# The SSD's y products of two pairs of heads run back to back, and the buffers around them change

## The chip, the cores and the metric

The kernel runs on one core of a Trainium2 chip. The metric is the device time of one execution in microseconds (us). A core has TensorE for matrix products (PE in the profile, PEld its loads of weights), VectorE (DVE), ScalarE (ACT), GpSimd (POOL), SyncE (SP), and DMA queues. Each engine works through its own instructions in the order in which the program has them; semaphores make one engine wait for another.

## The reference

One layer, float32, 272 tokens (16 meta tokens and 256 frames) of width 2048. What matters here is the SSD mixer in it: 64 heads of 64 channels in 8 groups, a state of 128.

```python
proj = xn @ w_in
sc_b, sc_c, sc_h, z, xbc, dt_raw, gate_raw = split_cols(proj, IN_SIZES)
xbc = jax.nn.silu(causal_dwconv(xbc, mb_conv_w, mb_conv_b))
xs, Bm, Cm = jnp.split(xbc, [D_INNER, D_INNER + D_BC], axis=-1)
...
decay = jnp.exp(jnp.where(causal, seg, -jnp.inf))
cb = jnp.einsum('bclgn,bcsgn->bcgls', Cc, Bc)
y_diag = jnp.einsum('bcgrls,bcsgrp->bclgrp', decay * cb[:, :, :, None], xdt)
...
y_m = (y_ssd + xs * d_skip[:, None].astype(xs.dtype)).reshape(bsz, L, D_INNER)
y_m = y_m * jax.nn.silu(z)
y_m = rmsnorm(y_m.reshape(bsz, L, MB_GROUPS, D_INNER // MB_GROUPS),
              mb_norm_g.reshape(MB_GROUPS, D_INNER // MB_GROUPS)).reshape(bsz, L, D_INNER)
```

After it come the two output projections, the gates, w_o, and an MLP of width 5504 with a convolution, all of which the change leaves alone. The kernel does the scan without chunks, as a masked product over all tokens: y = (decay * (C B)) x dt.

## The kernel before

Channels lie on the 128 partitions, tokens along the free dimension. A weight tile is 128 x 128; all products of the layer are one long list of jobs, and a job of the input projection is 16 such tiles, in two pieces of 8. A piece comes by DMA as float32 (raw), ScalarE rounds it to whi (line 115), VectorE computes the rest, wlo = raw - whi (line 116); PE then runs 16 matmuls with whi and 8 with wlo (lines 276 to 279). Four pairs of whi and wlo and five raw buffers run in a ring, so a cast for a piece waits until PE has finished the piece four before it.

The order on PE and on SP is the order in which the program is written. On the other engines a scheduler decides it when the program is built, and it is fixed then. What a job's result sets off later is put into a table by job number: after(delay, fn) runs fn when delay more jobs have been put on PE, ahead of that job's evacuation.

A group of eight heads (ssd_group, g = 0 to 7) has ten jobs: B, C, and four each of xs and z, alternating (in group 0 the z come earlier). A pair of heads fills 128 partitions, so a group has four pairs, i = 0 to 3. For pair i, after xs job: three jobs later xs_tr transposes xs on PE (L451, L452) into xd; one later decay(i) computes on GpSimd eight instructions (line 473) into the buffer m, from the rows qb that load_q brings; one later decay_exp(i) takes the exponential on ScalarE (L479) and multiplies by the masked C B, cbm, on VectorE (L480). Seven jobs after the xs job y_out(i) runs the y product on PE: for each of three blocks of tokens one matmul per head (L495), of 64 columns of weights each, into the two halves of one PSUM bank. The trace has two records for each of these float32 matmuls, so 12 for a pair. Then VectorE adds the skip (L497), GpSimd multiplies by silu(z) (L499), ScalarE squares, GpSimd adds the squares up in ss (L506). Two jobs after the last pair, y_norm sums ss over the partitions by a matmul on PE (ny, L512); VectorE and ScalarE make the reciprocal root of it, and GpSimd multiplies the group's four yf by it (L517). These steps of a group fall among the jobs of the next group. In the last group the delays are shorter.

The buffers: m has two, shared by all pairs; a decay can write one only after the y product that read it. qb has two, one per group. sqy, the square, has one.

Of the kernel before, what the change touches and what calls it, by code (L numbers as in the profile page):

```python
# [8 lines left out]
F32 = mybir.dt.float32  # L9
# [6 lines left out]
P = 128  # L16
# [3 lines left out]
T = SEQ + META  # L20
KD = D // P
HEADS = 64
GROUPS = 8
# [10 lines left out]
TR_DELAY, Y_DELAY = 3, 7  # L34
# [4 lines left out]
T_Y = 14  # L39
# [18 lines left out]
N0, N1, N2 = NY, T - 128, T - 256  # L58
NM = N0 + N1 + N2
L1 = 128 - T_Y  # L60
# [60 lines left out]
def block_kernel(ctx: ExitStack, tc: tile.TileContext, xT: bass.AP, par: bass.AP, w_in: bass.AP, w_a: bass.AP,  # L121
                 w_m: bass.AP, w_o: bass.AP, w_up: bass.AP, w_down: bass.AP, out: bass.AP):
    nc = tc.nc
# [39 lines left out]
    paux = ctx.enter_context(tc.tile_pool(name="paux", bufs=1, space=PSUM))  # L163
# [95 lines left out]
    def after(delay, fn):  # L259
        later.setdefault(state["job"] + delay, []).append(fn)  # L260
# [65 lines left out]
    sd = None  # L326
# [68 lines left out]
        after(5, transposes)  # L395

    def load_q(g):
        qb = sd.tile([P, 8, T], F32, tag="qb", name="qb", bufs=2)
        nc.gpsimd.dma_start(out=qb, in_=qd[8 * g:8 * g + 8, :].rearrange("h t -> (h t)").partition_broadcast(P)
                            .rearrange("p (h t) -> p h t", h=8))  # L400
        return qb

    def conv_silu(ps, j, c0, n, dst):

        e = sd.tile([P, T], F32, tag="e", name="e", bufs=2)
        nc.vector.tensor_tensor(out=e[:, c0:], in0=ps, in1=rstd[:, c0:], op=ALU.mult)
        a = 0 if c0 == 0 else T_Y
        u = sd.tile([P, T], F32, tag="u", name="u", bufs=2)
        nc.scalar.activation(out=u[:, a:], in_=e[:, a:], func=AF.Identity, scale=hc("mbw3", j), bias=hc("mbb", j))
        for s, w in ((1, "mbw2"), (2, "mbw1"), (3, "mbw0")):  # L410
            b = max(a, c0 + s)
            nc.vector.scalar_tensor_tensor(out=u[:, b:], in0=e[:, b - s:T - s], scalar=hc(w, j), in1=u[:, b:],
                                           op0=ALU.mult, op1=ALU.add)
        th = sd.tile([P, T], F32, tag="th", name="th", bufs=2)
        silu_of_half(dst[:, a:], u[:, a:], th[:, a:])

    def ssd_group(g):
        G = {}

        def b_evac(ps):  # L420
            G["B"] = Z["B"][g % 2]
            conv_silu(ps, 32 + g, 0, T, G["B"][:, :T])

        def c_evac(ps):
            G["C"] = sd.tile([P, T], F32, tag="C", name="C", bufs=2)
            conv_silu(ps, 40 + g, T_C, T - T_C, G["C"])
            after(2, cb)

        def cb():
            B, C = G["B"], G["C"]  # L430
            ps = paux.tile([P, 512], F32, tag="cb", name="cb")
            nc.tensor.matmul(ps[:, 0:N0], B[:, 0:128], C[:, T_Y:], start=True, stop=True)  # L432
            nc.tensor.matmul(ps[:, N0:N0 + N1], B[:, 128:256], C[:, 128:], start=True, stop=True)  # L433
            nc.tensor.matmul(ps[:, N0 + N1:NM], B[:, 256:], C[:, 256:], start=True, stop=True)  # L434
            m = G["cb"] = sd.tile([P, NM], F32, tag="cbm", name="cbm", bufs=2)
            nc.vector.tensor_tensor(out=m, in0=ps[:, :NM], in1=mask, op=ALU.mult)
            G["qb"] = load_q(g)

        def xs_evac(ps, i):
            j = 4 * g + i  # L440
            G["xs", i] = sd.tile([P, T], F32, tag=f"xs{i}", name="xs", bufs=2)
            conv_silu(ps, j, 0, T, G["xs", i])
            after(TR_DELAY if g < GROUPS - 1 else 2, lambda: xs_tr(i))
            after(Y_DELAY if g < GROUPS - 1 else 5, lambda: y_out(i))

        def xs_tr(i):
            j = 4 * g + i
            x = G["xs", i]
            ps = paux.tile([P, 512], F32, tag="tr", name="tr")
            for b in range(2):  # L450
                nc.tensor.transpose(ps[:, b * P:(b + 1) * P], x[:, b * P:(b + 1) * P], ident)  # L451
            nc.tensor.transpose(ps[:N2, 2 * P:3 * P], x[:, 256:], ident)  # L452
            xd = G["xd", i] = Z["xd"][i]
            tok = S["tok"]
            h = 2 * j
            nc.vector.tensor_tensor(
                out=xd[:, 0:2], in0=ps[:, :2 * P].rearrange("p (b h c) -> p b h c", b=2, h=2),
                in1=tok[:, :2 * HEADS].rearrange("p (b h) -> p b h", b=2)[:, :, h:h + 2].unsqueeze(3)
                .broadcast_to([P, 2, 2, 64]), op=ALU.mult)
            nc.vector.tensor_tensor(  # L460
                out=xd[:N2, 2], in0=ps[:N2, 2 * P:3 * P].rearrange("p (h c) -> p h c", h=2),
                in1=tok[:N2, 2 * HEADS + h:2 * HEADS + h + 2].unsqueeze(2).broadcast_to([N2, 2, 64]), op=ALU.mult)
            after(1, lambda: decay(i))

        def decay(i):
            tok, qb = S["tok"], G["qb"]
            m = G["m", i] = sd.tile([P, 2, NM], F32, tag="m", name="m", bufs=2)
            for a in range(2):
                hl = 2 * i + a
                h = 8 * g + hl  # L470
                q0, q1, q2, q0m = (tok[:, o * HEADS + h:o * HEADS + h + 1] for o in (3, 4, 5, 6))
                for c0, n, t0, q in ((0, L1, T_Y, q0), (L1, N1, 128, q0m), (N0, N1, 128, q1), (N0 + N1, N2, 256, q2)):
                    nc.gpsimd.tensor_scalar(out=m[:, a, c0:c0 + n], in0=qb[:, hl, t0:t0 + n], scalar1=q,  # L473
                                            scalar2=0.0, op0=ALU.subtract, op1=ALU.max)
            after(1, lambda: decay_exp(i))

        def decay_exp(i):
            m, cbm = G["m", i], G["cb"]
            nc.scalar.activation(out=m, in_=m, func=AF.Exp, scale=-1.0)  # L479
            nc.vector.tensor_tensor(out=m, in0=m, in1=cbm.unsqueeze(1).broadcast_to([P, 2, NM]), op=ALU.mult)  # L480

        def z_evac(ps, i):
            u = sd.tile([P, T], F32, tag="u", name="uz", bufs=2)[:, :NY]
            th = sd.tile([P, T], F32, tag="th", name="thz", bufs=2)[:, :NY]
            nc.vector.tensor_tensor(out=u, in0=ps, in1=rstdh[:, T_Y:], op=ALU.mult)
            G["sz", i] = sd.tile([P, NY], F32, tag=f"sz{i}", name="sz", bufs=1)
            silu_of_half(G["sz", i], u, th)

        def y_out(i):
            j = 4 * g + i  # L490
            xd, m = G["xd", i], G["m", i]
            y = paux.tile([P, 512], F32, tag="y", name="y", bufs=2)
            for b, c0, n, t0 in ((0, 0, N0, 0), (1, N0, N1, L1), (2, N0 + N1, N2, 256 - T_Y)):
                for a in range(2):
                    nc.tensor.matmul(y[64 * a:64 * a + 64, t0:t0 + n], xd[:, b, a, :], m[:, a, c0:c0 + n],  # L495
                                     start=b == 0, stop=b == 2)
            nc.vector.scalar_tensor_tensor(out=yf[j], in0=G["xs", i][:, T_Y:], scalar=pc("dskip", j), in1=y[:, :NY],  # L497
                                           op0=ALU.mult, op1=ALU.add)
            nc.gpsimd.tensor_tensor(out=yf[j], in0=yf[j], in1=G["sz", i], op=ALU.mult)  # L499
            if i == 0:  # L500
                G["ss"] = sd.tile([P, NY], F32, tag="ss", name="ss", bufs=1)
                nc.scalar.activation(out=G["ss"], in_=yf[j], func=AF.Square)
            else:
                sq = sd.tile([P, NY], F32, tag="sqy", name="sqy", bufs=1)
                nc.scalar.activation(out=sq, in_=yf[j], func=AF.Square)
                nc.gpsimd.tensor_tensor(out=G["ss"], in0=G["ss"], in1=sq, op=ALU.add)  # L506
            if i == 3:
                after(2 if g < GROUPS - 1 else 1, y_norm)

        def y_norm():  # L510
            ps = paux.tile([P, 512], F32, tag="misc", name="ny")[:, :NY]
            nc.tensor.matmul(ps, ones, G["ss"], start=True, stop=True)  # L512
            rs = sd.tile([P, NY], F32, tag="rs", name="rs", bufs=1)
            rsqrt_mean(rs, ps, 512, sd, "sqy")
            for i in range(4):
                j = 4 * g + i
                nc.gpsimd.tensor_tensor(out=yf[j], in0=yf[j], in1=rs, op=ALU.mult)  # L517

        in_product(J_B + g, 0, T, b_evac)
        in_product(J_C + g, T_C, T - T_C, c_evac)  # L520
        for b, i in group_order(g):
            if b == J_XS:
                in_product(b + 4 * g + i, 0, T, lambda ps, i=i: xs_evac(ps, i))
            else:
                in_product(b + 4 * g + i, T_Y, NY, lambda ps, i=i: z_evac(ps, i))
# [273 lines left out]
```

## Time and profile before

| | |
|---|---|
| median of 3 runs | 2131.57 us (2131.17 to 2131.7) |
| profiled execution | 2131.41 us |
| span of its instructions | 2129.7 us |
| PE busy | 2108.8 us, 99% of the span |
| PEld, DVE, ACT, POOL busy | 96%, 63%, 48%, 21% |
| mean granted TensorE clock | 0.997 of full speed |
| bytes read from HBM | 384.77 MB, 182 GB/s over the span |

The span runs from the first to the last instruction; the time of an execution has another 1.7 us around it. Busy shares are averages over the whole kernel. The SSD's groups run in the first 610 us of it; there POOL is busy for 314 us of the 540 between 60 and 600. Matmuls follow each other in a pipeline, so a record's duration is longer than the step to the next one; costs on PE are therefore read from starts. "L276 ... x8" in a timeline is eight records of that line in a row, merged, with the first one's start.

### The profile page before, as it was taken

How to read it: one execution, taken by the hardware profiler on the slowest of the kernel's cores; microseconds unless marked ns; L12 is line 12 of the kernel's file. 1: busy time of each engine (PE TensorE's matmuls, PEld its weight loads, DVE VectorE, ACT ScalarE, POOL GpSimd, SP SyncE). 2: the span in 40 equal slices, each digit the busy share in tenths (PEclk: the TensorE clock that was granted, in tenths of full speed). 3: DMA queues.
4: the chain of work that ended last, by engine and by line, in shares of the span. 5: the costliest groups of instructions: out<-in, count | busy, mean ns of one | idle time of the engine just before them, and what ended most of it. 6: DMA issues, size and time to landing. Idle time of an engine off the chain costs nothing.

```text
span 2129.7 us, 39486 instructions
## 1 busy us (share of the span) xinstructions
PE 2108.8 (99%) x16254; PEld 2035.5 (96%) x16254; DVE 1347.9 (63%) x1829; ACT 1015.6 (48%) x1317; POOL 449.8 (21%) x483
## 2 busy tenths in 40 slices
PE   8999999999999999999999999999999999999997
PEld 7999999999999999999999999999999999988887
DVE  8788888788774444555555555666666666655454
ACT  5455555555573333444444444555454454444442
POOL 4247555755710000000000002101111111100010
PEclk9999999999999999999999999999999999999999
DMA  7565555554446555555555556555555555556663
GB/s 235 199 196 178 164 184 180 180 180 159 158 159 202 185 182 185 182 186 180 187 180 186 180 184 222 182 184 184 183 188 182 185 185 182 188 180 184 192 188 118
DMA packets 108548, 389.50 MB, mean 183 GB/s; under 512 B 12352, under 2 KB 14656, under 8 KB 107344
## 3 DMA queue, kind: packets, MB, share of 16 engines
q1 hardware_dynamic: 105696, 374.96, 54.9%
q0 software_dynamic: 1952, 11.10, 1.5%
q8 instruction: 127, 2.08, 0.4%
q10 hardware_dynamic: 720, 0.93, 0.1%
q14 instruction: 53, 0.43, 0.1%
HBM read 384.77 MB, written 2.17 MB: 182 GB/s over the span
## 4 chain that ended last, share of the span: by engine, by line
PE 97%; DVE 1%; POOL 1%; issue 0%; ACT 0%; DVEq 0%; ACTq 0%; POOLq 0%
PE acc L279 32%; PE acc L277 24%; PE acc L276 24%; PE acc L274 15%; PE y L495 1%; DVE wlo L116 1%; PE tr L451 0%; POOL m L473 0%; DVE o L740 0%; PE cb L432 0%; PE ny L512 0%; PE tr L452 0%; POOL ss L506 0%; PE cb L433 0%; PE cb L434 0%
## 5 line engine op out<-in xcount | busy, mean ns | idle before, releaser
L115 ACT CAST whi<-raw 128x1024 fp32r<-128x1024 f32 (+1 forms) x724 | 744.5, 1030 | 971.9 <-PE acc L277 567.6
L116 DVE TENSOR_TENSOR wlo<-raw,whi 128x1024 fp32r<-128x1024 f32 (+1 forms) x724 | 883.1, 1221 | 453.3 <-ACT whi L115 426.9
L276 PE MATMUL acc<-xg,whi 128*128 128x258 f32 (+3 forms) x2576 | 646.2, 287 | 1.8 <-ACT whi L115 1.3
L277 PE MATMUL acc<-xg,whi 128*128 128x258 f32 (+3 forms) x2576 | 641.0, 284 | 3.6 <-DVE xg L205 3.6
L277 PEld LDWEIGHTS acc<-xg,whi 128*128 128x128 f32 x2576 | 485.1, 188 | 4.6 <-DVE xg L205 4.0
L276 PEld LDWEIGHTS acc<-xg,whi 128*128 128x128 f32 x2576 | 484.9, 188 | 3.4 <-ACT whi L115 2.4
L279 PE MATMUL acc<-xg,wlo 128*128 128x258 f32 (+3 forms) x2576 | 366.8, 284 | 3.1 <-DVE wlo L116 3.0
L279 PEld LDWEIGHTS acc<-xg,wlo 128*128 128x128 f32 x2576 | 335.6, 189 | 4.1 <-DVE wlo L116 4.1
L473 POOL TENSOR_SCALAR m<-qb,tok 128x144 f32<-128x144 f32 (+2 forms) x256 | 228.3, 909 | 108.1 <-PE y L495 100.3
L279 PE MATMUL acc<-hg,wlo 128*128 128x256 f32 (+1 forms) x1376 | 193.4, 283 | 0.0
L279 PEld LDWEIGHTS acc<-hg,wlo 128*128 128x128 f32 x1376 | 182.9, 189 | 7.5
L274 PE MATMUL acc<-hg,whi 128*128 128x512 f32 x688 | 175.0, 396 | 0.0
L277 PE MATMUL acc<-hg,whi 128*128 128x258 f32 x688 | 169.3, 285 | 0.0
L276 PE MATMUL acc<-hg,whi 128*128 128x258 f32 x688 | 169.2, 281 | 0.0
L274 PE MATMUL acc<-act,whi 128*128 128x512 f32 x645 | 163.0, 392 | 0.0
L686 POOL TENSOR_TENSOR u<-u,rs 128x256 f32<-128x256 f32 x43 | 57.6, 1339 | 431.6 <-ACT u L685 431.6
L274 PEld LDWEIGHTS acc<-hg,whi 128*128 128x128 f32 x688 | 123.8, 189 | 23.8
L274 PEld LDWEIGHTS acc<-act,whi 128*128 128x128 f32 x645 | 115.4, 189 | 19.8
L276 PEld LDWEIGHTS acc<-hg,whi 128*128 128x128 f32 x688 | 131.7, 191 | 0.0
L277 PEld LDWEIGHTS acc<-hg,whi 128*128 128x128 f32 x688 | 129.6, 188 | 0.0
L276 PE MATMUL acc<-ym,whi 128*128 128x258 f32 x512 | 125.5, 281 | 0.0
L277 PE MATMUL acc<-ym,whi 128*128 128x258 f32 x512 | 125.4, 284 | 0.0
(187 smaller groups left out, 2283.5 us busy)
## 6 DMA issues: line engine op xcount, KB each, us to landing
raw<-in_w_in_dram SPq DMA_DIRECT2D x316, 512.0 KB, 3.4
raw<-in_w_up_dram SPq DMA_DIRECT2D x172, 512.0 KB, 3.4
raw<-in_w_down_dram SPq DMA_DIRECT2D x80, 512.0 KB, 4.0
raw<-in_w_m_dram SPq DMA_DIRECT2D x64, 512.0 KB, 3.4
raw<-in_w_a_dram SPq DMA_DIRECT2D x32, 512.0 KB, 3.4
raw<-in_w_o_dram SPq DMA_DIRECT2D x32, 512.0 KB, 3.4
qb<-qd POOLq DMA_DIRECT2D x8, 1088.0 KB, 8.3
raw<-in_w_in_dram SPq DMA_DIRECT2D x12, 256.0 KB, 4.8
```

Of the source, the lines that this page charges most:

```text
L115: nc.scalar.copy(out=hi[:, :n], in_=r[:, :n])
L116: nc.vector.tensor_tensor(out=lo[:, :n], in0=r[:, :n], in1=hi[:, :n].bitcast(F32), op=ALU.subtract)
L274: nc.tensor.matmul(ps.rearrange("p (a n) -> p a n", a=2), wh, a, start=kk + k == 0, stop=False)
L276: nc.tensor.matmul(ps, wh, a[:, 0], start=kk + k == 0, stop=False)
L277: nc.tensor.matmul(ps, wh, a[:, 1], start=False, stop=False)
L279: nc.tensor.matmul(ps[:, :n], lo[:, k * P:(k + 1) * P], act[kk + k][:, 0, c0:c0 + n], start=False, stop=kk + k == nk - 1)
L473: nc.gpsimd.tensor_scalar(out=m[:, a, c0:c0 + n], in0=qb[:, hl, t0:t0 + n], scalar1=q, scalar2=0.0, op0=ALU.subtract, op1=ALU.max)
L495: nc.tensor.matmul(y[64 * a:64 * a + 64, t0:t0 + n], xd[:, b, a, :], m[:, a, c0:c0 + n], start=b == 0, stop=b == 2)
L686: nc.gpsimd.tensor_tensor(out=u, in0=u, in1=rs2[:, 2:], op=ALU.mult)
```

## The change

The y products of pairs 0 and 1 run together, where that of pair 1 stood, and those of 2 and 3 where that of 3 stood: y_out takes two pairs, issues the twelve matmuls, and then has both evacuated by y_evac. m gets four buffers, qb one, and the load of qb is written one job later (q_rows).

```diff
--- before.py
+++ after.py
@@ -395,7 +395,7 @@
         after(5, transposes)
 
     def load_q(g):
-        qb = sd.tile([P, 8, T], F32, tag="qb", name="qb", bufs=2)
+        qb = sd.tile([P, 8, T], F32, tag="qb", name="qb", bufs=1)
         nc.gpsimd.dma_start(out=qb, in_=qd[8 * g:8 * g + 8, :].rearrange("h t -> (h t)").partition_broadcast(P)
                             .rearrange("p (h t) -> p h t", h=8))
         return qb
@@ -434,6 +434,9 @@
             nc.tensor.matmul(ps[:, N0 + N1:NM], B[:, 256:], C[:, 256:], start=True, stop=True)
             m = G["cb"] = sd.tile([P, NM], F32, tag="cbm", name="cbm", bufs=2)
             nc.vector.tensor_tensor(out=m, in0=ps[:, :NM], in1=mask, op=ALU.mult)
+            after(1, q_rows)
+
+        def q_rows():
             G["qb"] = load_q(g)
 
         def xs_evac(ps, i):
@@ -441,7 +444,8 @@
             G["xs", i] = sd.tile([P, T], F32, tag=f"xs{i}", name="xs", bufs=2)
             conv_silu(ps, j, 0, T, G["xs", i])
             after(TR_DELAY if g < GROUPS - 1 else 2, lambda: xs_tr(i))
-            after(Y_DELAY if g < GROUPS - 1 else 5, lambda: y_out(i))
+            if i % 2:
+                after(Y_DELAY if g < GROUPS - 1 else 5, lambda: y_out(i - 1, i))
 
         def xs_tr(i):
             j = 4 * g + i
@@ -464,7 +468,7 @@
 
         def decay(i):
             tok, qb = S["tok"], G["qb"]
-            m = G["m", i] = sd.tile([P, 2, NM], F32, tag="m", name="m", bufs=2)
+            m = G["m", i] = sd.tile([P, 2, NM], F32, tag="m", name="m", bufs=4)
             for a in range(2):
                 hl = 2 * i + a
                 h = 8 * g + hl
@@ -486,14 +490,20 @@
             G["sz", i] = sd.tile([P, NY], F32, tag=f"sz{i}", name="sz", bufs=1)
             silu_of_half(G["sz", i], u, th)
 
-        def y_out(i):
+        def y_out(*pairs):
+            ys = [paux.tile([P, 512], F32, tag="y", name="y", bufs=2) for _ in pairs]
+
+            for i, y in zip(pairs, ys):
+                xd, m = G["xd", i], G["m", i]
+                for b, c0, n, t0 in ((0, 0, N0, 0), (1, N0, N1, L1), (2, N0 + N1, N2, 256 - T_Y)):
+                    for a in range(2):
+                        nc.tensor.matmul(y[64 * a:64 * a + 64, t0:t0 + n], xd[:, b, a, :], m[:, a, c0:c0 + n],
+                                         start=b == 0, stop=b == 2)
+            for i, y in zip(pairs, ys):
+                y_evac(y, i)
+
+        def y_evac(y, i):
             j = 4 * g + i
-            xd, m = G["xd", i], G["m", i]
-            y = paux.tile([P, 512], F32, tag="y", name="y", bufs=2)
-            for b, c0, n, t0 in ((0, 0, N0, 0), (1, N0, N1, L1), (2, N0 + N1, N2, 256 - T_Y)):
-                for a in range(2):
-                    nc.tensor.matmul(y[64 * a:64 * a + 64, t0:t0 + n], xd[:, b, a, :], m[:, a, c0:c0 + n],
-                                     start=b == 0, stop=b == 2)
             nc.vector.scalar_tensor_tensor(out=yf[j], in0=G["xs", i][:, T_Y:], scalar=pc("dskip", j), in1=y[:, :NY],
                                            op0=ALU.mult, op1=ALU.add)
             nc.gpsimd.tensor_tensor(out=yf[j], in0=yf[j], in1=G["sz", i], op=ALU.mult)
```

Lines behind the edits move: L473 becomes L477, L495 L500, L499 L509, L506 L516, L512 L522, L517 L527.

On PE, in the stretch where pair 1 of group 2 has its product (y is the PSUM bank, m the masked decays, xdz the pair's xd, tr the transposes of pair 3's xs):

```order
-L495 MATMUL y<-m,xdz_523 64x258 x2
-L495 MATMUL y<-m,xdz_523 64x144 x2
-L495 MATMUL y<-m,xdz_523 64x16 x2
-L451 MATMUL tr<-ident,xs 128x128 x2
-L452 MATMUL tr<-ident,xs 16x128
+L500 MATMUL y<-m,xdz_522 64x258 x2
+L500 MATMUL y<-m,xdz_522 64x144 x2
+L500 MATMUL y<-m,xdz_522 64x16 x2
+L500 MATMUL y<-m,xdz_523 64x258 x2
+L500 MATMUL y<-m,xdz_523 64x144 x2
+L500 MATMUL y<-m,xdz_523 64x16 x2
```

The product of pair 0 (xdz_522) has moved here from two jobs earlier; the transposes that stood behind pair 1's product stand behind both.

On GpSimd (POOL), around the end of a group: yf is the product with silu(z) of one pair, ss the sum of squares, m a decay of the next group. Before, from the second half of the decay that follows y3 to the group's first product with the norm:

```order
L473 TENSOR_SCALAR m<-qb,tok 128x114
L473 TENSOR_SCALAR m<-qb,tok 128x144 x2
L473 TENSOR_SCALAR m<-qb,tok 128x16
L499 TENSOR_TENSOR yf_1014<-yf_1014,sz 128x258
L506 TENSOR_TENSOR ss<-ss,sqy 128x258
L517 TENSOR_TENSOR yf_1011<-yf_1011,rs 128x258
```

Now, at the same place of the same group, from the second of the two decays that follow the run of y2 and y3 (the first, eight instructions, stands just ahead):

```order
L477 TENSOR_SCALAR m<-qb,tok 128x114
L477 TENSOR_SCALAR m<-qb,tok 128x144 x2
L509 TENSOR_TENSOR yf_1011<-yf_1011,sz 128x258
L477 TENSOR_SCALAR m<-qb,tok 128x16
L477 TENSOR_SCALAR m<-qb,tok 128x114
L477 TENSOR_SCALAR m<-qb,tok 128x144
L509 TENSOR_TENSOR yf_1012<-yf_1012,sz 128x258
L477 TENSOR_SCALAR m<-qb,tok 128x144
L477 TENSOR_SCALAR m<-qb,tok 128x16
L516 TENSOR_TENSOR ss<-ss,sqy 128x258
L399 DMA qb<-qd 128x2176
L516 TENSOR_TENSOR ss<-ss,sqy 128x258
```

The products yf of pairs 2 and 3 now stand inside the second decay, the ss of both behind it, and the load of the next group's rows between the two ss.

## Rows read from the trace of the kernel before

**Rows 1.** page, part 1: busy time, share of the span and instructions of each engine

```profile
PE 2108.8 (99%) x16254; PEld 2035.5 (96%) x16254; DVE 1347.9 (63%) x1829; ACT 1015.6 (48%) x1317; POOL 449.8 (21%) x483
```

**Rows 2.** page, part 4: the chain that ended last, by engine

```profile
PE 97%; DVE 1%; POOL 1%; issue 0%; ACT 0%; DVEq 0%; ACTq 0%; POOLq 0%
```

**Rows 3.** PE's waits: who waited for whom, us in total, times, longest

```profile
PE acc L277 <- DVE xg L205: 3.6, 2, 2.0
...
PE acc L276 <- DVE tok L380: 0.5, 1, 0.5
```

**Rows 4.** PE's timeline: start, us, engine, line, operation [idle before]; four steps between pieces

```profile
120.49 1.15 PE L279 MATMUL acc<-xg,wlo 128*128 128x262 f32 x8
122.78 0.37 PE L276 MATMUL acc<-xg,whi 128*128 128x272 f32 x1
...
159.08 1.12 PE L279 MATMUL acc<-xg,wlo 128*128 128x258 f32 x8
160.03 0.28 PE L276 MATMUL acc<-xg,whi 128*128 128x258 f32 x1
...
161.97 1.12 PE L279 MATMUL acc<-xg,wlo 128*128 128x258 f32 x8
163.17 0.37 PE L276 MATMUL acc<-xg,whi 128*128 128x272 f32 x1
...
596.71 1.13 PE L279 MATMUL acc<-xg,wlo 128*128 128x258 f32 x8
598.68 0.39 PE L276 MATMUL acc<-xg,whi 128*128 128x258 f32 x1
```

**Rows 5.** PE's timeline inside one y run, three narrow windows, from a pass's start

```profile
156.41 0.39 PE L495 MATMUL y<-m,xdz 128*64 128x258 f32 x2
...
156.63 0.42 PE L495 MATMUL y<-m,xdz 128*64 128x144 f32 x4
...
156.76 0.36 PE L495 MATMUL y<-m,xdz 128*64 128x144 f32 x6
```

**Rows 6.** PE's timeline, group 1: y3, and ny two products later

```profile
216.06 0.97 PE L495 MATMUL y<-m,xdz 128*64 128x258 f32 x12
...
229.43 0.60 PE L512 MATMUL ny<-ss,ones 128*128 128x258 f32 x2
```

**Rows 7.** POOL's timeline, group 1, from y3 to the last ss

```profile
217.18 6.43 POOL L473 TENSOR_SCALAR m<-qb,tok 128x114 f32<-128x114 f32 x8 [4.36 <-PE y L495]
223.57 0.75 POOL L499 TENSOR_TENSOR yf<-yf,sz 128x258 f32<-128x258 f32 x1
224.93 1.09 POOL L506 TENSOR_TENSOR ss<-ss,sqy 128x258 f32<-128x258 f32 x1 [0.61 <-ACT sqy L505]
```

**Rows 8.** page, part 5: the group of all decay instructions

```profile
L473 POOL TENSOR_SCALAR m<-qb,tok 128x144 f32<-128x144 f32 (+2 forms) x256 | 228.3, 909 | 108.1 <-PE y L495 100.3
```

**Rows 9.** POOL's timeline, a long decay, after a y1

```profile
256.07 8.23 POOL L473 TENSOR_SCALAR m<-qb,tok 128x114 f32<-128x114 f32 x8 [3.38 <-PE y L495]
```

**Rows 10.** PE's timeline, start of the kernel, then busy times and PEclk of one stretch

```profile
15.01 0.39 PE L277 MATMUL acc<-xg,whi 128*128 128x272 f32 x1 [1.97 <-DVE xg L205]
...
17.17 0.40 PE L277 MATMUL acc<-xg,whi 128*128 128x272 f32 x1 [1.64 <-DVE xg L205]
...
19.25 0.42 PE L276 MATMUL acc<-xg,whi 128*128 128x258 f32 x1
...
20.97 0.82 PE L279 MATMUL acc<-xg,wlo 128*128 128x258 f32 x4
...
18.00:21.40 3.40, 3.22 (x15) 3.22 (x16) 3.40 (x8) 0.62 (x1) 0.00 (x0) 0.50 0.64 185
```

**Rows 11.** timelines of POOL and PE, last group: its last ss, then ny

```profile
602.40 1.46 POOL L506 TENSOR_TENSOR ss<-ss,sqy 128x258 f32<-128x258 f32 x1 [1.74 <-ACT sqy L505]
...
604.56 0.60 PE L512 MATMUL ny<-ss,ones 128*128 128x258 f32 x2
```

**Rows 12.** page, part 6: DMA issues of the decays' rows, KB each, us to landing

```profile
qb<-qd POOLq DMA_DIRECT2D x8, 1088.0 KB, 8.3
```


## The prediction

> **What bounds the kernel now.** I read the page's busy times first: PE, TensorE's matmul side, is busy 99% of the span [rows 1]. The chain that ended last confirms it, 97% of it PE [rows 2]. The list of PE's waits then shows how little is left: seven rows from 3.6 us down to 0.5, 11.8 us in all, and neither a y product nor ny, the matmul that sums a group's squares, is among them [rows 3], of which the first and the last stand there. So only two things can change the time: how long PE's own instructions take, and whether PE begins to wait. VectorE, ScalarE, GpSimd (POOL) and the DMA queues matter only where PE's next operand comes from them.
>
> **The y products on PE.** In the timeline of PE a plain step between two pieces, from the first of eight wlo matmuls to the next piece's first matmul, is 160.03 - 159.08 = 0.95 us. With a y run between them it is 598.68 - 596.71 = 1.97, so a y run alone costs 1.02. With transposes alone it is 163.17 - 161.97 = 1.20, so those cost 0.25; with y and transposes 122.78 - 120.49 = 2.29, less a plain 0.97 and the 0.25 that makes 1.07 for y [rows 4]. What does a second y cost that follows the first directly? No row shows one, so I bound it. Above: 1.02, nothing saved. Below: the starts inside a run are 156.41, 156.63 and 156.76 [rows 5], that is 0.22 for each of two passes of 258 columns and 0.13 for each of two of 144; the 16-column ones add about 0.03 each. Sum 0.75, the price without entering or leaving, and I take that, because the operands of all twelve matmuls of the second y are there by then. Before, 26 of the 32 runs stand ahead of transposes or the cb products (1.07 each) and 6 alone (1.02): 33.9 us. After, by the new order on PE, 12 of 16 stand so and 4 alone, plus 16 second ones: 12.8 + 4.1 + 12.0 = 28.9. **Saved: 5.0 us**; bounds: nothing, and these 5.0.
>
> **What the moves do to POOL, and through it to PE.** The first y of each pair now runs two products later, with the second. In place of two m buffers there are four. A group's four decays need all four, so the next group's third and fourth decays (L477) cannot start until this group's second pair, y2 and y3, has run. Before, only one decay stood so: after y3, POOL ran one decay, then yf (L499), then ss (L506), and PE's ny came later than that. The order after puts both decays into POOL's queue ahead of most of the rest: sixteen decay instructions, the two yf products between the last of them, then ss, the load of qb, ss. PE's ny waits for the last ss, and everything on PE stands behind ny.
>
> The step before: y3 starts at 216.06, ny at 229.43, 13.37 us later [rows 6]. POOL's decay starts at 217.18, 1.12 after y3; eight instructions end at 223.61; yf takes 0.75; 0.61 goes to ScalarE's square; ss at 224.93 takes 1.09 and ends at 226.02, 3.4 us before ny [rows 7]. That spare is what two moves now use up.
>
> The step after, counted from the start of y2: PE is ready for ny at 13.37 + 0.75 = 14.1 us. POOL: 1.12 until the decay starts. Sixteen decay instructions: by the group of all 256, 228.3 us busy, 0.892 each [rows 8], 14.3. Two yf at 0.75: 1.5. The ss of pair 2: 1.09. Its square buffer is single, so ScalarE's square of pair 3 follows it: 0.61; the issue of the qb load falls beside that. The last ss: 1.09. Sum 1.12 + 14.3 + 1.5 + 1.09 + 0.61 + 1.09 = 19.7, and PE waits 19.7 - 14.1 = **5.6 us**. This comes once per group for groups 0 to 6, which have a group behind them: 7 x 5.6 = **39 us**. The bounds: with 6.43 for eight, as after y3 [rows 7], 18.3 and a wait of 4.2; with 8.23, the longest of the regular ones [rows 9], 21.9 and 7.8.
>
> [...]
>
> **The last group** has no decays behind it. Its ss ended at 602.40 + 1.46 = 603.86, ny started at 604.56 [rows 11], 0.7 to spare; ny comes 0.75 later now, and one more square and ss (0.61 and 1.46) come in between, with ScalarE's casts in their way. That is a wait of 0.5 to 1.6: **1 us**.
>
> **Edits I cost at nothing.** One qb buffer in place of two: the load can go only after the group's last decay, and lands 8.3 us after issue [rows 12]; the next decays wait anyway for the next group's first y pair, six products of about 6 us later. If that cover went, each group would add up to 8. The load's own program place moved a product later, and is hidden by the same. In group 0 the four decays run through without waiting for y (108.1 us of waits before decays, 100.3 on y, go or shrink [rows 8]); nobody on PE waits for them sooner, and ScalarE's exponentials, which stand between casts of weights, have their decays about as early as the casts need room. Cover gone, a us or two, once. The late first y of a pair finds its m and xd ready long before, and nobody needs its buffers sooner than the decays above. The exponentials of the two late decays hold back casts on ScalarE while PE stands at ny; PE has four pieces ready then, so nobody is late.
>
> **Sum** on the profiled execution's 2131.41 us (span 2129.7; 0.16 under the median 2131.57): -5.0 + 39 + 10.5 + 1 = +45.5, so **2177 us**, 2.1% slower.
>
> **The rivals.** *The clock holds.* The gaps do not drop it: 2131.4 + 35 = 2166. For it: the trace shows only two gaps close together doing it. Against: each new gap is longer than both together. 0.17.
>
> *POOL is slower or the clock stays low longer*, 8.2 us for each decay, the casts behind ScalarE's exponentials late as well: 7 x 7.8 + 7 x 1.5 - 5.0 + 1.6 = +62, 2193; with 3 us of clock each, 2204. For it: some take 8.23 [rows 9]. Against: those after y3 took 6.43. 0.18.
>
> *Faster: POOL keeps up.* If the ss chain ends within 14.1 us, PE never waits and the 5.0 us stay: 2126, 0.24% faster. It decides at sixteen decays in 14.1 - 1.12 - 4.3 = 8.7 us, 0.54 each. Against: the mean is 0.892 and the quickest of the regular eights 6.43. For: only if the decays started before y2 and y3 end, in a buffer freed sooner. 0.04.
>
> *Nothing happens.* A second y costs 1.02 as well and POOL just keeps up: 2131.6. It needs the same 8.7 us. 0.02.
>
> **How the numbers follow.** The forecast itself, gaps of 4.2 to 7 us with some loss of clock, gets 0.59: 2165 to 2190. The range takes in the clock that holds, down to the shortest gap with nothing lost behind it, 2131.4 - 5 + 29 + 1 = 2156, and most of the slow rival, up to 2200; outside are the rest of that, and the two cases without a gap. A measurement tells about 0.2%, 4.3 us, from no change. Slower by more than that: 0.59 + 0.17 + 0.18 = 0.94. Within: 0.02. Faster: 0.04.
>
> **What would show it.** In the profile after: PE ny waiting for POOL ss, seven times, some 5 to 6 us each, at the head of PE's waits; GpSimd's decays in two runs of eight back to back after each group's second y run; a granted clock of 0.5 for some us behind each gap; y's records 24 in a run of under 1.8 us. If no such wait is there, the chain on POOL is wrong; if the waits are there and the clock is whole, the price behind them is wrong; if y's runs take twice 1.02, the saving is.

## The result, and the profile after

The changed kernel takes **2185.65 us** (median of 5 runs, 2184.82 to 2186.56) against 2131.57 (2129.65 to 2131.92, 5 runs) before: slower, by a ratio of 1.0256, 95% interval 1.0244 to 1.0267, or 54.1 us. The profiled execution took 2185.65 us with a span of 2183.9; the mean granted clock is 0.985 of full speed, where it was 0.997.

The page after, its busy times, chain (by engine, by line) and the group of the decays:

```profile
PE 2121.3 (97%) x16254; PEld 2048.0 (94%) x16254; DVE 1346.3 (62%) x1829; ACT 1017.2 (47%) x1317; POOL 448.5 (21%) x483
...
PE 90%; POOL 7%; DVE 1%; ACT 1%; issue 1%; DMA 0%; DVEq 0%; SPq 0%; ACTq 0%
PE acc L279 29%; PE acc L277 22%; PE acc L276 22%; PE acc L274 14%; POOL m L477 6%; PE y L500 1%; POOL yf L509 1%; DVE wlo L116 1%; PE ny L522 0%; POOL ss L516 0%; ACT m L483 0%; DVE o L750 0%; PE tr L455 0%; DVE xg L205 0%; DMA gain<-in_par_dram 0%
...
L477 POOL TENSOR_SCALAR m<-qb,tok 128x144 f32<-128x144 f32 (+2 forms) x256 | 221.7, 883 | 185.6 <-PE y L500 177.5
```

PE has as many instructions as before and stands idle for more of the span [rows 1]. The chain, 97% PE before [rows 2], has 7% POOL now, nearly all of it decays: not the ss that PE waits for, but what stands ahead of it in POOL's queue. The decays are no slower than they were, 883 ns against 909 [rows 8]; their idle time behind y has grown from 100.3 to 177.5 us, in fewer and longer waits (14 in place of 23): there are half as many y runs, and two decays stand behind each. So POOL has no more work, and its busy share is the same 21%; it does the same work at the wrong time.

PE's waits after (who waited for whom: us in total, times, longest), the first and third of the list:

```profile
PE ny L522 <- POOL ss L516: 41.4, 7, 6.7
...
PE tr L455 <- DVE xdz L464: 1.7, 1, 1.7
```

Before, the longest line was 3.6 us and ny was not listed [rows 3]. One such wait in the timelines of group 1, PE first, from y2 and y3 to ny:

```profile
223.66 1.77 PE L500 MATMUL y<-m,xdz 128*64 128x258 f32 x24
...
243.77 1.23 PE L522 MATMUL ny<-ss,ones 128*128 128x258 f32 x2 [5.75 <-POOL ss L516]
```

and POOL between the same two points:

```profile
224.75 9.12 POOL L477 TENSOR_SCALAR m<-qb,tok 128x114 f32<-128x114 f32 x11 [9.57 <-PE y L500]
233.84 1.48 POOL L509 TENSOR_TENSOR yf<-yf,sz 128x258 f32<-128x258 f32 x1
235.31 3.19 POOL L477 TENSOR_SCALAR m<-qb,tok 128x16 f32<-128x16 f32 x3
238.46 1.42 POOL L509 TENSOR_TENSOR yf<-yf,sz 128x258 f32<-128x258 f32 x1
239.87 1.27 POOL L477 TENSOR_SCALAR m<-qb,tok 128x144 f32<-128x144 f32 x2
241.10 0.73 POOL L516 TENSOR_TENSOR ss<-ss,sqy 128x258 f32<-128x258 f32 x1
241.77 0.62 POOL L399 DMA_DIRECT2D qb<-qd  x1
242.77 0.95 POOL L516 TENSOR_TENSOR ss<-ss,sqy 128x258 f32<-128x258 f32 x1 [0.37 <-ACT sqy L515]
```

POOL idles 9.57 us until the y run frees its buffers, then works without a pause through sixteen decays (9.12 + 3.19 + 1.27 = 13.6 us), with the two yf between them, and has the last ss done 20 us after y2 began. PE had been ready for ny 5.75 us before it could start.

The clock around this gap and around that of group 2 (columns: window, us, busy us and instructions of each engine, granted clock PEclk, DMA share, GB/s):

```profile
237.40:243.00 5.60, 0.62 (x6) 0.34 (x4) 3.66 (x7) 2.65 (x6) 5.23 (x8) 1.00 0.66 189
243.00:249.80 6.80, 6.03 (x25) 5.84 (x26) 3.62 (x5) 2.45 (x3) 0.71 (x1) 0.50 0.48 165
249.80:256.00 6.20, 6.20 (x52) 6.20 (x52) 4.70 (x7) 2.48 (x3) 3.59 (x4) 1.00 0.29 90
...
314.60:321.40 6.80, 3.56 (x14) 3.38 (x15) 3.72 (x4) 3.22 (x5) 2.81 (x5) 0.50 0.71 231
```

PE works for 0.62 of the first 5.60 us; then the granted clock is 0.50, and PE gets through 25 matmuls in 6.8 us where the next 6.2 us have 52. In group 2 the low stretch begins earlier against the gap (ny starts at 317.84, by PE's timeline), so half of it falls on time in which PE stood anyway. Around the first gap, that of group 0, the granted clock is 0.50 for longer, from 171.3 to 181.5.

### The profile page after: what moved, and what is told of

It reads as the page before. It is cut to its first block, busy times and chain, and to the rows that moved or that the text cites. A ratio compares the mean times of both kernels' runs of the same rounds, so it can differ in the third digit from the quotient of the medians.

```text
span 2183.9 us, 39480 instructions
## 1 busy us (share of the span) xinstructions
PE 2121.3 (97%) x16254; PEld 2048.0 (94%) x16254; DVE 1346.3 (62%) x1829; ACT 1017.2 (47%) x1317; POOL 448.5 (21%) x483
## 3 DMA queue, kind: packets, MB, share of 16 engines
q1 hardware_dynamic: 105696, 374.96, 53.5%
## 4 chain that ended last, share of the span: by engine, by line
PE 90%; POOL 7%; DVE 1%; ACT 1%; issue 1%; DMA 0%; DVEq 0%; SPq 0%; ACTq 0%
PE acc L279 29%; PE acc L277 22%; PE acc L276 22%; PE acc L274 14%; POOL m L477 6%; PE y L500 1%; POOL yf L509 1%; DVE wlo L116 1%; PE ny L522 0%; POOL ss L516 0%; ACT m L483 0%; DVE o L750 0%; PE tr L455 0%; DVE xg L205 0%; DMA gain<-in_par_dram 0%
## 5 line engine op out<-in xcount | busy, mean ns | idle before, releaser
L276 PE MATMUL acc<-xg,whi 128*128 128x258 f32 (+3 forms) x2576 | 655.5, 290 | 2.1 <-ACT whi L115 1.5
L277 PE MATMUL acc<-xg,whi 128*128 128x258 f32 (+3 forms) x2576 | 649.3, 287 | 3.6 <-DVE xg L205 3.6
L277 PEld LDWEIGHTS acc<-xg,whi 128*128 128x128 f32 x2576 | 492.1, 191 | 5.0 <-DVE xg L205 4.1
L276 PEld LDWEIGHTS acc<-xg,whi 128*128 128x128 f32 x2576 | 492.0, 191 | 3.9 <-ACT whi L115 2.4
L477 POOL TENSOR_SCALAR m<-qb,tok 128x144 f32<-128x144 f32 (+2 forms) x256 | 221.7, 883 | 185.6 <-PE y L500 177.5
```

The source lines that it names most:

```text
L276: nc.tensor.matmul(ps, wh, a[:, 0], start=kk + k == 0, stop=False)
L277: nc.tensor.matmul(ps, wh, a[:, 1], start=False, stop=False)
```

## The experiments

The theory was the prediction's: the pairing puts sixteen decays ahead of the last ss on POOL, PE stands at ny for it, and the clock falls behind each stand. The rivals: the new buffers are to blame, or the y products themselves became dearer, or the stands cost only their own length. Medians of before beside the runs were 2131.43 us (2129.72 to 2132.15, 21 runs) for the first four, 2131.23 (2129.77 to 2132.09, 33 runs) for the next four and 2131.18 (2129.73 to 2132.28, 21 runs) for the last two.

**1. The norm two products later** (changed kernel):

```diff
-                after(2 if g < GROUPS - 1 else 1, y_norm)
+                after(4 if g < GROUPS - 1 else 1, y_norm)
```

> The changed kernel with y_norm two jobs later (delay 4 in place of 2), nothing else. Theory: PE's seven waits of 5.9 us at ny come because the group's last ss leaves POOL about 20 us after y2 starts, while PE reaches ny after 14; two more jobs put 12 us between, so the waits go to 0, the clock stays up, and what is left is the saving on PE: 2185.7 - 41.4 - 17 = 2127, a ratio to the kernel before of 0.998. Rival, the buffers: the single qb or the m buffers hold PE up in another place, then the time stays above 2140 and the wait moves to a y product. Rival, the y runs themselves are dear: it stays above 2135 without any wait.

Measured: 2127.89 us (2126.79 to 2129.32, 11 runs), ratio 0.9985 (0.9976 to 0.9993); the clock is 0.996, and ny is gone from PE's waits. Its POOL still runs the decays, yf and ss in the same order as above. One number in the table of delays takes back all of the 54 us: y was not dearer, PE only came to ny too early.

**2. The other end: POOL's order.** The norm stays; the third decay of a group is put behind the last ss of the group ahead (follow orders two instructions for the scheduler):

```diff
-                    nc.gpsimd.tensor_scalar(out=m[:, a, c0:c0 + n], ...
+                    one = nc.gpsimd.tensor_scalar(out=m[:, a, c0:c0 + n], ...
+                    if i == 2 and g > 0:
+                        follow(one, S["ss", g - 1])
...
-                nc.gpsimd.tensor_tensor(out=G["ss"], in0=G["ss"], in1=sq, op=ALU.add)
+                S["ss", g] = nc.gpsimd.tensor_tensor(out=G["ss"], in0=G["ss"], in1=sq, op=ALU.add)
```

> The changed kernel with one ordering edge on POOL: a group's third decay (i = 2) stands behind the last ss of the group before; delays and buffers as in the change. Theory: the wait at ny is the order of POOL's queue alone, so it goes to 0 (ss would end some 6 us after y3) and the time is 2127, ratio 0.998, the same as with ny later. Rival, the ss chain is late for another reason (VectorE's evacuation, ScalarE's squares): waits of several us stay and the time is over 2150.

Measured: 2128.36 us (2126.79 to 2129.8, 11 runs), ratio 0.9986 (0.9977 to 0.9995), no wait at ny. POOL's timeline in group 1 of this kernel:

```profile
218.66 1.55 POOL L511 TENSOR_TENSOR yf<-yf,sz 128x258 f32<-128x258 f32 x2 [10.48 <-DVE yf L509]
220.17 0.74 POOL L518 TENSOR_TENSOR ss<-ss,sqy 128x258 f32<-128x258 f32 x1
221.49 1.46 POOL L518 TENSOR_TENSOR ss<-ss,sqy 128x258 f32<-128x258 f32 x1 [0.57 <-ACT sqy L517]
222.93 14.99 POOL L477 TENSOR_SCALAR m<-qb,tok 128x114 f32<-128x114 f32 x16
```

The same sixteen decays, 15 us of them, now stand behind the ss, and nobody on PE needs them soon. Runs 1 and 2 undo the loss independently, one at the waiter, one at the queue ahead of what it waits for.

**3. The gap kept, the clock held.** Products that nothing reads are put into the gap, ahead of ny in groups 0 to 6:

```diff
-            ps = paux.tile([P, 512], F32, tag="misc", name="ny")[:, :NY]
+            full = paux.tile([P, 512], F32, tag="misc", name="ny")
+            ps = full[:, :NY]
+            for _ in range(24 if g < GROUPS - 1 else 0):
+                nc.tensor.matmul(full[:, 384:], ones, ones, start=True, stop=True)
```

> The changed kernel with 24 products of ones by ones, 128 columns, on PE just ahead of ny in groups 0 to 6, written to columns of ny's bank that nobody reads; about 0.22 us each, 5.3 us in all, so PE works where it waited. [...] Rival: the clock costs nothing and only the waits do: it stays at 2186 or, where the products overrun, above.

By the theory the wait at ny falls to about 0.6 us a group and only what the low clock cost comes back, by my estimate the 17 us that 2185.7 - 41.4 leaves above 2127: 2169.

Measured: 2170.83 us (2170.53 to 2172.26, 4 runs), ratio 1.0187 (1.0173 to 1.0201), clock 0.996. The 24 products took 5.52 us in group 1, 0.23 each. PE's wait at ny, and then the two windows that hold the gap and the low stretch above:

```profile
PE ny L525 <- POOL ss L516: 4.0, 7, 1.3
```

```profile
237.00:243.00 6.00, 5.61 (x49) 5.41 (x48) 4.01 (x7) 2.96 (x5) 5.27 (x7) 1.00 0.71 211
243.00:249.80 6.80, 6.80 (x55) 6.76 (x54) 4.88 (x8) 2.52 (x3) 1.14 (x2) 1.00 0.50 163
```

PE still waits a little for ss, so the added products do not hold ny up; the granted clock stays 1.00. The difference to the changed kernel, 2185.65 - 2170.83 = **14.8 us**, is what the clock costs, 2.1 for each gap. The two profiled executions agree: from the ny of group 0 to that of the last group there are 658.98 - 175.99 = 482.99 us in the changed kernel and 645.25 - 177.35 = 467.90 in this one, 15.1 less. The rest, 39.4 us over before, is the gaps themselves less the saving. PE's timelines of one period, from the ny of one group to the next, put the three parts beside each other. Before, then run 1, then run 3, then the changed kernel (from group 2 to group 3, in run 3 from 1 to 2; its next period, to 385.34, is 71.33):

```profile
295.23 0.60 PE L512 MATMUL ny<-ss,ones 128*128 128x258 f32 x2
...
361.00 0.60 PE L512 MATMUL ny<-ss,ones 128*128 128x258 f32 x2
```

```profile
305.13 0.60 PE L522 MATMUL ny<-ss,ones 128*128 128x258 f32 x2
...
370.42 0.60 PE L522 MATMUL ny<-ss,ones 128*128 128x258 f32 x2
```

```profile
242.69 0.70 PE L525 MATMUL ny<-ss,ones 128*128 128x258 f32 x2 [0.39 <-POOL ss L516]
...
314.01 0.70 PE L525 MATMUL ny<-ss,ones 128*128 128x258 f32 x2 [0.39 <-POOL ss L516]
```

```profile
317.84 1.23 PE L522 MATMUL ny<-ss,ones 128*128 128x258 f32 x2 [5.74 <-POOL ss L516]
...
390.81 1.23 PE L522 MATMUL ny<-ss,ones 128*128 128x258 f32 x2 [5.74 <-POOL ss L516]
```

Before 65.77 us; with the pairing and no gap 65.29, so the pairing saves 0.48 a group; with the gap 71.32, so a gap costs 6.03; with the clock 72.97 here and 317.84 - 243.77 = 74.07 in the period ahead, so the clock costs 1.65 and 2.75. The smaller one follows the gap of group 2, where half of the low stretch fell on idle time.

**4. The pairing without the buffers.** The changed kernel with the old buffers and the load at its old place:

```diff
-        qb = sd.tile([P, 8, T], F32, tag="qb", name="qb", bufs=1)
+        qb = sd.tile([P, 8, T], F32, tag="qb", name="qb", bufs=2)
...
-            after(1, q_rows)
-
-        def q_rows():
             G["qb"] = load_q(g)
...
-            m = G["m", i] = sd.tile([P, 2, NM], F32, tag="m", name="m", bufs=4)
+            m = G["m", i] = sd.tile([P, 2, NM], F32, tag="m", name="m", bufs=2)
```

> The pairing of the y products alone, with the buffers and the load of the kernel before (two m, two qb, load with cb). Theory: what puts two decays between y2, y3 and their ss is that both come free in one place, whatever the number of buffers; with two m buffers the next two decays wait for the same run, so the gaps at ny are there too, 5 to 7 us each for at least the groups 1 to 6, and the time is 2175 to 2195. Rival, the buffers are to blame: 2127 to 2135.

Measured: 2183.95 us (2182.14 to 2185.41, 4 runs), ratio 1.0247 (1.0233 to 1.0261), and the same wait:

```profile
PE ny L519 <- POOL ss L513: 41.4, 7, 6.7
```

The buffers have no part in the gaps. With two buffers it is the next group's first two decays that wait for y2 and y3, with four its last two; sixteen instructions either way. The wait of 1.7 us at the transposes isn't there.

**5. The buffers without the pairing.** The same three edits the other way round, in the kernel before:

```diff
-        qb = sd.tile([P, 8, T], F32, tag="qb", name="qb", bufs=2)
+        qb = sd.tile([P, 8, T], F32, tag="qb", name="qb", bufs=1)
...
+            after(1, q_rows)
+
+        def q_rows():
             G["qb"] = load_q(g)
...
-            m = G["m", i] = sd.tile([P, 2, NM], F32, tag="m", name="m", bufs=2)
+            m = G["m", i] = sd.tile([P, 2, NM], F32, tag="m", name="m", bufs=4)
```

> Before, with the buffers of the change alone: four for the masked decays, one for the decay's rows, the load of the rows a job later; the y products stay one by one. Theory (the gaps come from the pairing, through the decays that must wait for two y products of the group ahead): no wait of PE at ny, time within 2 us of before, 2130 to 2134, perhaps with the wait of the transposes on xdz of 1.3 to 1.7 us in group 0 that the profile of the change shows. Rival (the single buffer of rows delays the decays, so the buffers have a part in the gaps): PE waits at ny, some us a group, 2145 or more.

Measured: 2134.12 us (2132.75 to 2135.47, 10 runs), ratio 1.0014 (1.0005 to 1.0023): 2.9 slower, just past the upper end of what was expected, so the edits that I had costed at nothing cost something. PE's waits show where:

```profile
PE tr L454 <- DVE xdz L463: 1.8, 1, 1.8
```

How it comes about can be read in the changed kernel, group 0, in the timelines of ScalarE, VectorE and PE:

```profile
114.90 0.90 ACT L483 ACTIVATE m<-m 128x836 f32<-128x836 f32 x1 [3.63 <-POOL m L477]
...
115.84 1.03 DVE L484 TENSOR_TENSOR m<-m,cbm 128x836 f32<-128x836 f32 x1 [2.58 <-ACT m L483]
...
127.77 0.27 DVE L464 TENSOR_TENSOR xdz<-tr,tok 16x128 f32<-16x128 f32 x1
...
128.18 0.41 PE L455 MATMUL tr<-ident,xs 128*128 128x128 f32 x2 [1.70 <-DVE xdz L464]
```

With four buffers the decays of group 0 run through, and the scheduler puts all four of their exponentials ahead of 116 us, where run 10, with two, has two. ScalarE stands 3.63 us for the last of them and VectorE 2.58 for its product; from there VectorE works without a pause up to this xdz, and PE's transposes wait for it. The other 1.1 us of this run I did not place.

**6. The norm only one product later** (changed kernel):

```diff
-                after(2 if g < GROUPS - 1 else 1, y_norm)
+                after(3 if g < GROUPS - 1 else 1, y_norm)
```

> The changed kernel with the norm's matmul three products behind the second pair instead of two. A product is about 6.0 us of PE, and the waits at ny were 5.7 to 6.7 us. Theory (PE arrives at ny too early, by the length of POOL's queue, and everything else follows): the wait shrinks to 0 to 0.7 us a group, no stretch of low clock behind it, 2128 to 2132. Rival (one product later brings other work of POOL ahead of the last ss, as the scheduler orders anew): waits of 2 us or more a group stay, 2140 or more.

Measured: 2131.23 us (2129.02 to 2131.81, 10 runs), ratio 1.0 (0.9991 to 1.0009). Two waits are left:

```profile
PE ny L522 <- POOL ss L516: 1.3, 2, 0.9
```

and the five other groups have none. A product of 6 us takes away waits of 5.7 to 6.7 whole or but for a rest of 0.9 and 0.4: the dose fits. This kernel has no margin, and no gain either. Of the 3.3 us to run 1, 1.3 is this; the start of the profiled execution was also 2.0 us later (PE's wait for tok ends at 48.79, in run 1 at 46.82), but whether that holds for the median is not shown.

**7 and 8. The pairing with the old buffers, mended at either end**: run 4 with the norm four products later (the diff of run 1),

> The pairing alone, with two buffers for the masked decays, two for the rows, their load at its old place, and the norm four products later. Theory (the buffers of the change bring nothing; its one buffer of rows costs 1.3 us in group 0, at the transposes' wait on xdz): 2126 to 2127, 1 to 1.5 us under the same with the buffers of the change (2127.9). Rival (with two buffers a pair's decays can't run ahead, so y waits for exponentials): waits at y, 2130 or more.

and run 4 with the edge of run 2, laid on the first decay of a group, which is the one that waits with two buffers:

```diff
-                    if i == 2 and g > 0:
+                    if i == 0 and g > 0:
                         follow(one, S["ss", g - 1])
```

> The pairing alone with the old buffers, and on POOL the decays of pair 0 of a group placed behind the last sum of squares of the group ahead; the norm stays two products behind. Theory (only POOL's order sets the gaps): no wait of PE at ny, 2126 to 2128. Rival (with two buffers the decays so held back come too late for their y): waits of PE at y, 2131 or more.

Measured: the first 2126.84 us (2125.59 to 2127.89, 11 runs), ratio **0.9979** (0.997 to 0.9988), with no wait at y, ny or the transposes; the second 2129.62 (2127.78 to 2132.17, 11 runs), ratio 0.9994 (0.9985 to 1.0003), with one wait at ny:

```profile
PE ny L521 <- POOL ss L515: 2.0, 1, 2.0
```

It stands in the last group, whose delays are shorter and which the edge on POOL doesn't help. So the second missed its forecast of 2126 to 2128 by 1.6 us; the forecast had no wait at ny. The first beats both kernels.

**9. Is the gain the pairing's?** The kernel before with the diff of run 1 alone:

> The kernel before, with y one pair at a time, and only the norm's matmul four products behind the last pair instead of two. Theory (the 4.4 us that the pairing gains once the norm stands later are the y products' own, entered 16 times instead of 32): PE had no wait at ny before, so nothing changes, 2130 to 2132. Rival (the later norm itself brings the gain, by some order of POOL, VectorE or ScalarE behind it): 2126 to 2129.

Measured: 2131.8 us (2130.57 to 2132.76, 11 runs), ratio 1.0004 (0.9995 to 1.0013): nothing. The 4.4 us of run 7 are the pairing's own.

**10. Which buffer makes the wait of group 0?** The first kernel of run 7 with one buffer for the rows:

```diff
-        qb = sd.tile([P, 8, T], F32, tag="qb", name="qb", bufs=2)
+        qb = sd.tile([P, 8, T], F32, tag="qb", name="qb", bufs=1)
```

> The pairing with the norm four products later, two buffers for the masked decays, and one for the decay's rows, loaded at the old place. Theory (the wait of the transposes on xdz in group 0 comes from the four buffers of the masked decays, which let decays 2 and 3 and their exponentials run earlier): no wait of tr on xdz, 2126 to 2128. Rival (the single buffer of rows makes it): the wait of 1.3 to 1.8 us is there, 2128 or more, or decays late for y, with waits of PE at y.

Measured: 2127.23 us (2126.07 to 2128.15, 10 runs), ratio 0.9982 (0.9973 to 0.9991); no wait of the transposes. One qb buffer costs nothing that can be told (0.4 us, less than the runs differ among themselves). What is left for the 1.3 to 1.8 us are the four m buffers or the later load. In group 0 the load was not in fact later. POOL's timeline in the changed kernel and then in this one, the store of qd and the load of its rows into qb:

```profile
74.36 0.74 POOL L371 DMA_DIRECT2D qd<-dt_q  x1 [27.69 <-DVE dt_q0m L369]
76.81 0.58 POOL L399 DMA_DIRECT2D qb<-qd  x1 [1.70 <-DMA qd<-dt_q]
```

```profile
75.62 0.75 POOL L371 DMA_DIRECT2D qd<-dt_q  x1 [27.69 <-DVE dt_q0m L369]
78.06 0.57 POOL L399 DMA_DIRECT2D qb<-qd  x1 [1.70 <-DMA qd<-dt_q]
```

It is issued 2.45 us after the store in the one and 2.44 in the other, since it waits for the store in both. That points at the four m buffers; no run has them with the load at its old place, so it is argued and not shown.

## Why the prediction was right, point by point

The forecast was 2177 us, slower, in 2156 to 2200; 2185.65 came, by the mechanism that was named. Its terms:

- **The wait at ny, 39 us: 41.4.** Right in place, number and engine. Per group 5.6 was forecast, and 5.7 to 6.7 came. That the sum came so near is in part luck, since errors inside it offset each other: sixteen decays took 13.6 us, not 14.3, and the two ss 0.73 and 0.95, not 1.09, but each yf took 1.4 to 1.5, not the 0.75 of [rows 7]. The period of run 3 adds that a gap costs 6.03 where its wait is 5.75. The reason as I put it, that four buffers make the next group's third and fourth decays wait, is only half of it: run 4 has two buffers and the same 41.4. Pairing the y products is enough, since two buffers then come free at once, late.
- **The clock, 10.5 us: 14.8.** This is the step that was sized too low. I took 1.5 us for every gap, an estimate from the kernel's start: in its low stretch of 3.4 us, at a granted clock of 0.50, eight matmuls of 258 columns took 20.97 - 19.25 = 1.72 us where eight take 0.95 [rows 4, 10], 0.096 more for each of some 16. No run shows that term behind a gap. The rows above show 6.8 us at 0.50, 10.2 around the first gap, and run 3 gives 2.1 a gap, between the nothing and the 3 us of the rivals. So the half of the slow rival in which the clock stays low longer came true, and its slow decays did not. That a single gap of 5.75 us is enough to lower the clock, which no row of before showed, is shown now; the rival in which the clock holds (2166) is out. With PE kept at work through the gap in run 3 the granted clock stayed 1.00 (237.00 to 249.80 us); with PE idle there in the changed kernel it fell to 0.50 (243.00 to 249.80).
- **The saving, -5.0 us: -4.4** by runs 7 and 9 (interval 2.6 to 6.4). The second y in a run is a little dearer than the 0.75 of its passes. In PE's timeline after, a run without transposes and the plain steps around it:

```profile
154.19 1.15 PE L279 MATMUL acc<-xg,wlo 128*128 128x272 f32 x8
155.27 1.77 PE L500 MATMUL y<-m,xdz 128*64 128x258 f32 x24
156.97 0.39 PE L276 MATMUL acc<-xg,whi 128*128 128x258 f32 x1
```

  The step is 156.97 - 154.19 = 2.78, less a plain 0.98 is 1.80, less the 1.02 of a single y [rows 4] is 0.78.
- **The last group, 1 us: nothing.** PE has no wait at ny there. The last ss ends 0.69 us before ny, and before it was 0.70: on POOL at 656.82 + 1.47 = 658.29, and ny starts at 658.98. The square that I had added ran ahead of a cast on ScalarE (655.38, 1.05 long) behind which the last square stood; before, the only square stood behind one too (600.96, 1.05 long). Runs that order POOL or the other engines anew can have one (2.0 in run 8), so the spare of 0.7 [rows 11] is as thin as I said.
- **The edits costed at nothing:** one qb buffer indeed (run 10). The wait of 1.7 us at the transposes did come; runs 5 and 10 put it on the buffers, and the four m, by which the decays of group 0 run through, are the likely part of them. The text had "a us or two, once" as the price if the cover went.

Together, with 14.8 and 4.4 from medians and the rest from the profiled executions: 41.4 + 14.8 + 1.7 - 4.4 = 53.5 of the 54.2 us between the spans. Two smaller things nearly cancel: the 0.28 by which a gap costs more than its wait, 2.0 in all, and the start, where PE's wait for tok (L380) ended at 48.35 us before and at 46.67 after, -1.7, in work that the change doesn't touch.

## What to carry to other kernels

An order that makes one engine's instructions cheaper also moves the moment at which it frees buffers; look at which queue refills them, and what short instruction stands behind that refill. Here 0.5 us a group was saved on TensorE and 8 lost, because two buffers came free at once and sixteen instructions were served ahead of the one that TensorE needed next. Two cures work at different ends: let the consumer come later (run 7, the best kernel of this study), or hold the refill behind the short instruction (run 2).

## What the runs showed of the hardware

Single gaps of 5.75 and 5.74 us, on a TensorE that was busy for 97% of the span, set the granted clock to 0.50 for the 6.8 us of either window shown, which cost 2.75 and 1.65 us on top of the gap, the less where half of the low stretch fell into the gap itself. One wait of 2.0 us, at ny in run 8, did not slow the matmuls behind it: those of 258 columns started 0.12 us apart (601.16, 601.28, 601.40), as they had ahead of it (597.05, 597.17, 597.29). Matmuls whose result nobody reads, put into the gap, kept the granted clock at 1.00 (run 3, 237.00 to 249.80 us) and gave back 14.8 us of the 54: where PE had to wait here, it was better kept at work. And entering and leaving the half-width y products cost 1.02 - 0.78 = 0.24 us each time, a little less than the 1.02 - 0.75 = 0.27 that the sum of the passes gave.
